# Loading the input of a nearest-neighbour upsampling as eight blocks of one 16 KiB descriptor per partition, in place of four of 32 KiB

## The chip, the cores and the metric

The kernel runs on one core of one Trainium2 chip; the other cores do nothing. The metric is the device time of an execution in microseconds (us). A kernel has two times here. The *time* is that of an execution as it was measured for the comparison (199.99 us for the kernel before, median of three runs). The *span* is what the profile of one execution covers, from the first instruction to the last (198.2 us for the same kernel); it is 1.8 us shorter.

Three words are used throughout. A *descriptor* is the order to move one contiguous run of bytes. In these traces every load and store shows one data *packet* for each descriptor, of the descriptor's size. A *semaphore* is a counter by which one unit tells another that its work is done.

## The reference

```python
x = random, shape (16, 64, 64, 64), float32; scale_factor = 2
for i in range(new_h):
    for j in range(new_w):
        result[:, :, i, j] = x[:, :, i // 2, j // 2]
```

Every element is written four times, to a square of two by two. There is no arithmetic: 16.78 MB are read, 67.11 MB are written.

## The kernel before

The input has 65,536 rows of 64 numbers. They are taken in four blocks of 128 partitions times 128 rows, each loaded with one DMA; a partition's 128 rows are contiguous in memory, 32 KiB. Each block is expanded in four steps of 32 rows. VectorE (DVE) copies 18 of the rows and ScalarE (ACT) 14, reading through a broadcast pattern that repeats rows and columns; the result, 32 KiB per partition, is stored with one DMA. There are two output buffers. All loads and all stores are issued by SyncE (SP), so they stand on one queue.

```python
K, J = 32, 4
NB = R // (P * J * K)                      # 4
xf = x.rearrange("b c h w -> (b c h) w").rearrange("(n p r) w -> n p r w", n=NB, p=P)
of = ...                                   # the same blocks of the output
KV = 18
xpool = ctx.enter_context(tc.tile_pool(name="xin", bufs=NB))
upool = ctx.enter_context(tc.tile_pool(name="uexp", bufs=2))
xts = []
for n in range(NB):
    xt = xpool.tile([P, J * K, W], fdt, name="xt")
    nc.sync.dma_start(out=xt[:, :, :], in_=xf[n])
    xts.append(xt)
...
for n in range(NB):
    for j in range(J):
        r0 = j * K
        u = upool.tile([P, K, s, W, s], fdt, name="u")
        nc.vector.tensor_copy(out=u[:, :KV], in_=expanded(xts[n][:, r0 : r0 + KV, :]))
        nc.scalar.copy(out=u[:, KV:], in_=expanded(xts[n][:, r0 + KV : r0 + K, :]))
        nc.sync.dma_start(out=of[n, :, r0 : r0 + K, :], in_=u[:, :, :, :, :])
```

A small function, `begin_before_barrier`, moves the first load ahead of the program's opening barrier. The change leaves it alone.

Of the kernel before, what the change touches and what calls it, by code (L numbers as in the profile page):

```python
# [1 line left out]

# [4 lines left out]


def begin_before_barrier(nc):



    blocks = nc.main_func.blocks
    main, body = blocks[0], blocks[1]
    sp = mybir.EngineType.SP
    load = next(i for i in body.instructions if i.engine == sp)
    assert isinstance(load, mybir.InstDMACopy), type(load)
    assert not (load.sync_info and load.sync_info.on_wait)
    body.instructions = [i for i in body.instructions if i is not load]
    kept = list(main.instructions)  # L20
    at = next(
        n
        for n, i in enumerate(kept)
        if i.engine == sp and isinstance(i, mybir.InstDrain)
    )
    kept.insert(at, load)
    main.instructions = kept


@with_exitstack  # L30
def kernel(
    ctx: ExitStack,
    tc: tile.TileContext,
    x: bass.AP,
    scale_factor: int,
    out: bass.AP,
):
    nc = tc.nc
    nc.at_finalize(begin_before_barrier)
    P = nc.NUM_PARTITIONS  # L40
    s = int(scale_factor)
    B, C, H, W = x.shape
    R = B * C * H
    fdt = x.dtype




    K, J = 32, 4
    NB = R // (P * J * K)  # L50
    assert NB * P * J * K == R
    xf = x.rearrange("b c h w -> (b c h) w").rearrange(
        "(n p r) w -> n p r w", n=NB, p=P
    )
    of = out.rearrange("b c (h hd) w -> (b c h) (hd w)", hd=s).rearrange(
        "(n p r) w -> n p r w", n=NB, p=P
    )

    KV = 18

    xpool = ctx.enter_context(tc.tile_pool(name="xin", bufs=NB))
    upool = ctx.enter_context(tc.tile_pool(name="uexp", bufs=2))

    xts = []
    for n in range(NB):
        xt = xpool.tile([P, J * K, W], fdt, name="xt")
        nc.sync.dma_start(out=xt[:, :, :], in_=xf[n])
        xts.append(xt)

    def expanded(rows):  # L70
        k = rows.shape[1]
        return rows.unsqueeze(2).unsqueeze(4).to_broadcast([P, k, s, W, s])

    for n in range(NB):
        for j in range(J):
            r0 = j * K
            u = upool.tile([P, K, s, W, s], fdt, name="u")
            nc.vector.tensor_copy(  # L78
                out=u[:, :KV], in_=expanded(xts[n][:, r0 : r0 + KV, :])
            )  # L80
            nc.scalar.copy(  # L81
                out=u[:, KV:], in_=expanded(xts[n][:, r0 + KV : r0 + K, :])
            )
            nc.sync.dma_start(
                out=of[n, :, r0 : r0 + K, :], in_=u[:, :, :, :, :]
            )


# [1 line left out]
_INS = ['x', 'scale_factor']  # L90
_OUTS = [((16, 64, 128, 128), 'float32')]

_NUMBERS = {'scale_factor': 2}


# [26 lines left out]
```

## Time and profile before

| | before |
|---|---|
| time, median of 3 runs | 199.99 us |
| span of the profiled run | 198.2 us |
| share of 16 DMA engines' span filled | 98.8% |
| DVE, ACT busy | 21%, 26% |
| data packets of the 16 engines | 2560 of 32 KiB, median 1213 ns |
| first load lands, first store issued, first store's packets start | 12.3, 15.6, 41.4 us |

These lines are from the page of the kernel before. The two rows of 40 entries cut the span into equal slices: the DMA row gives the busy share of the engines in tenths, the GB/s row what they moved. The last line is the chain of waits in shares of the span.

```profile
span 198.2 us, 145 instructions
...
DVE 40.9 (21%) x16; ACT 52.0 (26%) x17; POOL 0.2 (0%) x4
...
DMA  8999999999999999999999999999999999999994
GB/s 317 423 423 430 450 430 456 370 403 423 423 423 436 436 443 456 436 436 423 423 423 423 423 443 443 450 450 436 423 423 423 423 423 436 436 443 456 436 436 212
...
q1 hardware_dynamic: 2880, 83.89, 98.8%
...
DMA 77%; ACT 14%; issue 0%; ACTq 0%
...
```

The DMA engines are full in every slice but the first and the last. DVE and ACT are idle three quarters of the time, which speaks against either as the limit. Below is the beginning of the chain of waits in order of time: start, duration, and what the chain was in.

```profile
...
0.00 12.32 DMA xt<-in_x_dram
...
12.35 6.27 ACT u L81 x2
...
18.63 43.02 DMA out_dram<-u
...
61.75 3.19 ACT u L81
...
```

This view invites a mistake. It opens with 12.3 us of waiting for the first load and 6.3 us of copies, and one would think that a load half as large saves 5 us. But look at what follows: 43 us "in a store". Four MiB take a store only about 9.7 us of DMA. The timeline (start, duration, engine, instruction, and in brackets the idle time before it and what ended that) shows the same stretch:

```profile
...
0.00 2.15 SPq L67 DMA_DIRECT2D xt<-in_x_dram  x4
...
12.35 6.26 ACT L81 COPY u<-xt 128x3584 f32<-128x3584 f32 x2 [10.28 <-DMA xt<-in_x_dram]
...
15.55 40.05 SPq L84 DMA_DIRECT2D out_dram<-u  x3
52.07 3.18 ACT L81 COPY u<-xt 128x3584 f32<-128x3584 f32 x1 [33.47 <-DMA out_dram<-u]
...
```

The first store is issued at 15.55 us, but its buffer is free, so that the third copy can start, only at 52.07 us. It stands on the same queue behind all four loads, and those take until about 41 us. The store was ready some 26 us before the engines could turn to it. Finally, the windows view (second column: length; then busy times with counts, clock, DMA share and GB/s) of the two microseconds in which reads give way to writes:

```profile
...
39.00:41.00 2.00, 0.00 (x0) 0.00 (x0) 0.00 (x0) 1.00 0.94 262
...
```

Here the rate drops to 262 GB/s, the one dip after the start. The view counts a packet's bytes where the packet starts, and 16 packets of 32 KiB in 2 us are just 262 GB/s, so the figure is coarse.

### The profile page before, as it was taken

How to read it: one execution, taken by the hardware profiler on the slowest of the kernel's cores; microseconds unless marked ns; L12 is line 12 of the kernel's file. 1: busy time of each engine (PE TensorE's matmuls, PEld its weight loads, DVE VectorE, ACT ScalarE, POOL GpSimd, SP SyncE). 2: the span in 40 equal slices, each digit the busy share in tenths (PEclk: the TensorE clock that was granted, in tenths of full speed). 3: DMA queues.
4: the chain of work that ended last, by engine and by line, in shares of the span. 5: the costliest groups of instructions: out<-in, count | busy, mean ns of one | idle time of the engine just before them, and what ended most of it. 6: DMA issues, size and time to landing. Idle time of an engine off the chain costs nothing.

```text
span 198.2 us, 145 instructions
## 1 busy us (share of the span) xinstructions
DVE 40.9 (21%) x16; ACT 52.0 (26%) x17; POOL 0.2 (0%) x4
## 2 busy tenths in 40 slices
DVE  0055000000405050505050505050505050404000
ACT  2057000000415150606060606060606060505000
POOL 0000000000000000000000000000000000000000
DMA  8999999999999999999999999999999999999994
GB/s 317 423 423 430 450 430 456 370 403 423 423 423 436 436 443 456 436 436 423 423 423 423 423 443 443 450 450 436 423 423 423 423 423 436 436 443 456 436 436 212
DMA packets 2880, 83.89 MB, mean 423 GB/s; under 512 B 320, under 2 KB 320, under 8 KB 320
## 3 DMA queue, kind: packets, MB, share of 16 engines
q1 hardware_dynamic: 2880, 83.89, 98.8%
HBM read 16.78 MB, written 67.11 MB: 423 GB/s over the span
## 4 chain that ended last, share of the span: by engine, by line
DMA 77%; ACT 14%; issue 0%; ACTq 0%
DMA out_dram<-u 70%; ACT u L81 14%; DMA xt<-in_x_dram 6%; ACTq L81 0%
## 5 line engine op out<-in xcount | busy, mean ns | idle before, releaser
L81 ACT COPY u<-xt 128x3584 f32<-128x3584 f32 x16 | 50.8, 3179 | 128.3 <-DMA out_dram<-u 118.0
L78 DVE COPY u<-xt 128x4608 f32<-128x4608 f32 x16 | 40.9, 2560 | 139.6 <-DMA out_dram<-u 127.3
L81 ACT ACT_TABLE_LOAD x1 | 1.3, 1283 | 0.8 <-PEq L103 0.8
L103 POOL MEMSET const-bfloat16-1.0<- 128x1 bf16 x1 | 0.1, 102 | 0.0
L103 POOL MEMSET const-uint8-127<- 128x1 uint8 x1 | 0.1, 102 | 0.0
L103 POOL MEMSET const-float32-0.0<- 128x1 f32 x1 | 0.1, 99 | 0.2 <-issue 0.2
L103 POOL MEMSET const-float32-1.0<- 128x1 f32 x1 | 0.1, 99 | 0.0
## 6 DMA issues: line engine op xcount, KB each, us to landing
out_dram<-u SPq DMA_DIRECT2D x16, 4096.0 KB, 16.1
xt<-in_x_dram SPq DMA_DIRECT2D x4, 4096.0 KB, 25.9
```

The lines of the kernel that those rows point to most:

```text
L78: nc.vector.tensor_copy(out=u[:, :KV], in_=expanded(xts[n][:, r0 : r0 + KV, :]))
L81: nc.scalar.copy(out=u[:, KV:], in_=expanded(xts[n][:, r0 + KV : r0 + K, :]))
L103: nc = _bacc.Bacc("TRN2", target_bir_lowering=False, num_devices=1)
```

## The change

The intent is to start earlier: eight blocks of 64 rows per partition, each in a tile of its own, loaded with one descriptor of 16 KiB per partition. The first copies can begin after 2 MiB instead of 4 MiB. Stores, copies and the split between DVE and ACT stay as they are.

```diff
+    blocks = [64, 64, 64, 64, 64, 64, 64, 64]
-    K, J = 32, 4
-    NB = R // (P * J * K)
+    K = 32
...
+    def of_block(rows, first, k):
+        return rows[first : first + P * k, :].rearrange("(p k) w -> p k w", p=P)
-    xpool = ctx.enter_context(tc.tile_pool(name="xin", bufs=NB))
+    xpool = ctx.enter_context(tc.tile_pool(name="xin", bufs=1))
...
-    for n in range(NB):
-        xt = xpool.tile([P, J * K, W], fdt, name="xt")
-        nc.sync.dma_start(out=xt[:, :, :], in_=xf[n])
-        xts.append(xt)
+    for n, k in enumerate(blocks):
+        xt = xpool.tile([P, k, W], fdt, name=f"x{n}")
+        nc.sync.dma_start(out=xt[:, :, :], in_=of_block(xf, first, k))
+        loaded.append((xt, first, k))
+        first += P * k
...
-    for n in range(NB):
-        for j in range(J):
-            r0 = j * K
+    for xt, first, k in loaded:
+        for r0 in range(0, k, K):
...
-                out=of[n, :, r0 : r0 + K, :], in_=u[:, :, :, :, :]
+                out=of_block(of, first, k)[:, r0 : r0 + K, :],
+                in_=u[:, :, :, :, :],
```

More of the change, by code (lines that the diff above doesn't have):

```diff
@@ L44 @@
     fdt = x.dtype
-    K, J = 32, 4
-    NB = R // (P * J * K)
-    assert NB * P * J * K == R
-    xf = x.rearrange("b c h w -> (b c h) w").rearrange(
-        "(n p r) w -> n p r w", n=NB, p=P
-    )
-    of = out.rearrange("b c (h hd) w -> (b c h) (hd w)", hd=s).rearrange(
-        "(n p r) w -> n p r w", n=NB, p=P
-    )
-    KV = 18
-    xpool = ctx.enter_context(tc.tile_pool(name="xin", bufs=NB))
-    upool = ctx.enter_context(tc.tile_pool(name="uexp", bufs=2))
-    xts = []
-    for n in range(NB):
-        xt = xpool.tile([P, J * K, W], fdt, name="xt")
-        nc.sync.dma_start(out=xt[:, :, :], in_=xf[n])
-        xts.append(xt)
@@ L70, in expanded @@
-    def expanded(rows):
-        k = rows.shape[1]
-        return rows.unsqueeze(2).unsqueeze(4).to_broadcast([P, k, s, W, s])
-    for n in range(NB):
-        for j in range(J):
-            r0 = j * K
+    blocks = [64, 64, 64, 64, 64, 64, 64, 64]
+    K = 32
+    assert P * sum(blocks) == R
+    KV = 18
+    xf = x.rearrange("b c h w -> (b c h) w")
+    of = out.rearrange("b c (h hd) w -> (b c h) (hd w)", hd=s)
+    def of_block(rows, first, k):
+        return rows[first : first + P * k, :].rearrange("(p k) w -> p k w", p=P)
@@ new lines @@
+    xpool = ctx.enter_context(tc.tile_pool(name="xin", bufs=1))
+    upool = ctx.enter_context(tc.tile_pool(name="uexp", bufs=2))
+    loaded = []
+    first = 0
+    for n, k in enumerate(blocks):
[3 more added lines that the diff above has]
+        first += P * k
+    def expanded(rows):
+        return rows.unsqueeze(2).unsqueeze(4).to_broadcast(
+            [P, rows.shape[1], s, W, s]
+        )
@@ L77 @@
+    for xt, first, k in loaded:
+        for r0 in range(0, k, K):
             u = upool.tile([P, K, s, W, s], fdt, name="u")
             nc.vector.tensor_copy(
-                out=u[:, :KV], in_=expanded(xts[n][:, r0 : r0 + KV, :])
+                out=u[:, :KV], in_=expanded(xt[:, r0 : r0 + KV, :])
             )
             nc.scalar.copy(
-                out=u[:, KV:], in_=expanded(xts[n][:, r0 + KV : r0 + K, :])
+                out=u[:, KV:], in_=expanded(xt[:, r0 + KV : r0 + K, :])
```

## The prediction

> **What bounds the kernel.** The 16 DMA engines, from start to end. The page's slices show DMA at 0.8 in the first, 0.9 or more in the next 38, 0.4 in the last; the queue fills 98.8% of 16 engines' span. DVE is busy 21%, ACT 26%. Each of the 2560 data packets (512 of loads, 2048 of stores) carries 32 KiB; almost all take 1213 ns, so 160 per engine are 194.1 us of the 198.2 us span. The rest is 1.0 us before the first packet, about 0.7 us extra in each engine's first packet, about 1.0 us extra in the last two load packets, where reads give way to writes (the windows show 262 GB/s at 39 to 41 us), 0.2 us of semaphore packets (9 ns each) and 1.4 us of tail.
>
> The chain of waits seems to say otherwise: it starts with 12.3 us of the first load, then 6.3 us of ACT copies. But the stores released there stand on the same queue, behind all four loads: the first was issued at 15.6 us, started at 41.4 us when the loads had drained, and freed its buffer at 52.1 us. From there a store's 9.7 us of DMA is the period; the copies (3.18 us ACT, 2.56 us DVE) finish 6 us before the store ahead of them lands.
>
> **What the change does.** Bytes, stores, copies and buffers stay. Four loads of 32 KiB per partition become eight of 16 KiB.
> - Removed: half of the first wait. The first load lands at about 7.4 us, the first store is issued near 10.6 us. Worth nothing: it still stands behind loads that keep the queue busy until about 41 us.
> - Added: four issues on SP, 0.33 to 0.50 us each; all eight in about 4.3 us. A half load is 4.85 us of DMA, so the queue never runs dry. Hidden.
> - Added: four semaphore packets per engine, 9 ns each: 0.04 us, on the critical resource.
> - Added: 32 data packets per engine. The Trainium skill (DMA: Bandwidth & Descriptors, "Where 436 GB/s comes from") gives a ceiling of 435.2 GB/s, 1205 ns for 32 KiB on one of 16 engines; the trace has 1213 ns, and 1208 ns from start to start. So a packet's fixed cost is some 4 to 8 ns (estimate from these): 0.1 to 0.3 us.
> - Moved: a store's output runs lie 64 KiB apart between partitions, not 128 KiB, still 32 KiB long; I expect 1213 ns still.
> - Unsure: the read-to-write stretch costs 1 us in two 32 KiB packets. If it holds two packets whatever their size, up to 0.5 us may go.
>
> All of it is on the critical resource, and all is small: +0.2 us from packets, minus an uncertain 0.1.
>
> **Predicted: 200.1 us**, 199.5 to 200.8 (8 in 10). Faster by over 2%: 0.02; within 2%: 0.96; slower: 0.02.
>
> **What shows it right or wrong.** First copies start at 7 to 8 us, first store issued near 10.6 us; the third copy still starts near 52 us, the last near 178 us; DMA share stays near 98.8%; 3456 packets; load packets take 605 to 612 ns, stores 1213 ns; the first wait in the chain halves while the next DMA piece grows by the same 5 us.
>
> **What would make it wrong.** Load packets well above 612 ns; stores above 1213 ns through the new row pitch; stores overtaking the loads, so that reads and writes mix and the dip vanishes or spreads; a queue that holds fewer than eight loads, delaying the stores until DMA idles.

## The result

| | before | after |
|---|---|---|
| time, median of 4 runs each | 200.01 us (199.96 to 200.46) | 199.73 us (199.68 to 199.93) |
| span of the profiled run | 198.21 us | 198.00 us |
| first copies start | 12.35 us | 7.85 us |
| first store issued | 15.55 us | 11.05 us |
| third copies start | 52.07 us | 52.15 us |
| last copies start | 177.92 us | 177.95 us |
| last data packet ends | 196.82 us | 196.85 us |
| from there to the end of the span | 1.39 us | 1.16 us |

The ratio is 0.9983, with a 95% interval of 0.9966 to 1.0: the same at a limit of 2%, and perhaps a quarter of a microsecond faster. Ratios here are the mean time of one kernel's runs over the mean of the other's runs of the same rounds, so they are not quite the ratios of the medians in the tables. Executions over 1.5% slower than the fastest of the same kernel are left out of the means. The results are correct.

The page after:

```profile
span 198.0 us, 149 instructions
...
DMA  8999999999999999999999999999999999999995
GB/s 268 434 434 434 430 427 430 424 427 424 424 424 437 444 463 430 437 430 430 424 424 424 424 437 444 457 437 430 437 430 424 424 424 424 437 437 463 437 430 232
DMA packets 3456, 83.89 MB, mean 424 GB/s; under 512 B 384, under 2 KB 384, under 8 KB 384
...
q1 hardware_dynamic: 3456, 83.89, 99.0%
...
DMA 77%; ACT 14%; issue 0%; ACTq 0%
...
```

There are 3456 packets in place of 2880: 512 more of data and 64 more for semaphores. The engines are as full as before, and the chain's shares have hardly moved. The chain of waits in order of time:

```profile
...
0.00 7.82 DMA x<-in_x_dram
...
7.85 6.27 ACT u L83 x2
...
14.13 47.54 DMA out_dram<-u
...
61.77 3.19 ACT u L83
...
```

The first wait shrank from 12.32 to 7.82 us, and the 43.02 us in the store grew to 47.54 us. The 4.5 us that were won at the start were given back one line later. The timeline says the same:

```profile
...
0.00 4.32 SPq L68 DMA_DIRECT2D x<-in_x_dram  x8
...
7.85 6.26 ACT L83 COPY u<-x 128x3584 f32<-128x3584 f32 x2 [5.77 <-DMA x<-in_x_dram]
...
11.05 44.64 SPq L86 DMA_DIRECT2D out_dram<-u  x3
52.15 3.18 ACT L83 COPY u<-x 128x3584 f32<-128x3584 f32 x1 [38.05 <-DMA out_dram<-u]
...
```

The first store is issued 4.5 us earlier, and the third copy starts at 52.15 us, where it started at 52.07. The windows view over the same two microseconds:

```profile
...
39.00:41.00 2.00, 0.00 (x0) 0.00 (x0) 0.00 (x0) 1.00 1.00 344
...
```

Reads now give way to writes at 344 GB/s, not 262. The packet records confirm a gain in these two profiles: the last 64 KiB of loads of each engine, until its first store, took 2.89 us in place of 3.41. But the beginning was slower. In the same records, the first 2 MiB of loads took 5.73 us from the first packet until the first packet of the next 2 MiB, against 5.46 us before. The six stretches of 2 MiB between the first and the last took 4.87 us each on average, against 4.84. (From the first packets' starts: 6.74 to 35.95 us after, 6.47 to 35.51 before, divided by six.) The sum is about even. From the mean start of the 16 earliest load packets to the mean start of the 16 earliest store packets it is 40.37 us before and 40.38 us after. (A later profile of the changed kernel gave 40.16 us, so 0.2 us of this is chance. The records do not name a packet's engine; counted in another way these figures move by some hundredths, and a recorded expectation below has 40.34 and 40.17 us where this count gives 40.38 and 40.21.)

So where do the 0.2 us between the two spans come from? From the last line of the table: the last data packets end together (196.82 and 196.85 us), but the program ends 0.23 us sooner after them. The waits of SP's queue show it, as one line each (waited for whom: us in total, times, longest). Before:

```profile
...
SPq L117 <- DMA out_dram<-u: 15.7, 1, 15.7
...
```

After:

```profile
...
SPq L120 <- DMA out_dram<-u: 15.5, 2, 9.6
...
```

The line number is that of the program's end, where SP waits for the semaphores of all DMAs. Before, there was one wait for a DMA, after there are two. The records of the single waits make it plain. The DMAs take eight semaphores in rotation, and the closing waits go through them in a fixed order:

```
us, closing waits of SP
before                                     after
197.165  wait 104   (the last store's)     181.530  wait 104
197.224  wait 105, 103                     181.588  wait 105, 103
197.285  wait 106, 100                     181.650  wait 106, 100
197.349  wait 107, 99                      187.536  wait 107, 99
197.411  wait 108, 102                     197.207  wait 108, 102   (108 the last store's)
197.476  the queue's drain                 197.272  the queue's drain
```

With 20 DMAs the last store is on the fourth semaphore, number 104, which is waited for first. Everything else then follows at 0.06 us each, after the last store has landed. With 24 DMAs the last store is on the eighth, 108, which is waited for last; the other waits were over long before. Four instructions of 0.06 us (197.165 to 197.411 us) account for the difference. They have nothing to do with loads, except that there are four more of them.

### The profile page after: what moved, and what is told of

It is laid out like the page before. It is cut to its first block, busy times and chain, and to the rows that moved or that the text cites. A ratio compares the mean times of both kernels' runs of the same rounds, so it can differ in the third digit from the quotient of the medians.

```text
span 198.0 us, 149 instructions
## 1 busy us (share of the span) xinstructions
DVE 40.9 (21%) x16; ACT 52.0 (26%) x17; POOL 0.2 (0%) x4
## 2 busy tenths in 40 slices
DMA packets 3456, 83.89 MB, mean 424 GB/s; under 512 B 384, under 2 KB 384, under 8 KB 384
## 3 DMA queue, kind: packets, MB, share of 16 engines
q1 hardware_dynamic: 3456, 83.89, 99.0%
## 4 chain that ended last, share of the span: by engine, by line
DMA 77%; ACT 14%; issue 0%; ACTq 0%
DMA out_dram<-u 73%; ACT u L83 14%; DMA x<-in_x_dram 4%; ACTq L83 0%
## 5 line engine op out<-in xcount | busy, mean ns | idle before, releaser
L83 ACT COPY u<-x 128x3584 f32<-128x3584 f32 x16 | 50.8, 3179 | 128.3 <-DMA out_dram<-u 122.5
L80 DVE COPY u<-x 128x4608 f32<-128x4608 f32 x16 | 40.9, 2560 | 139.7 <-DMA out_dram<-u 131.8
```

The source lines that it names most:

```text
L80: nc.vector.tensor_copy(out=u[:, :KV], in_=expanded(xt[:, r0 : r0 + KV, :]))
L83: nc.scalar.copy(out=u[:, KV:], in_=expanded(xt[:, r0 + KV : r0 + K, :]))
```

## The experiments

The main theory has two parts. (1) The DMA engines are full, and the stores stand behind the loads; so the earlier landing is worth nothing, and the smaller descriptors come out even. (2) The 0.2 us that were won belong to the number of DMAs, through the closing waits. The rivals: the smaller descriptors, or the earlier start, made the gain; and, for (1), the order on the one queue holds back a gain that is there to be had.

Every experiment was timed in five rounds beside the kernel before on the same chip. All are correct in their results. Below, "loads" is the time from the mean start of the 16 earliest load packets to the mean start of the 16 earliest store packets, and "tail" the time from the end of the last data packet to the end of the span, both from the profiled run.

### Small descriptors without more DMAs: four_16k

The blocks of the changed kernel, loaded in pairs, so one DMA carries two 16 KiB descriptors per partition.

```diff
-        xt = xpool.tile([P, k, W], fdt, name=f"x{n}")
-        nc.sync.dma_start(out=xt[:, :, :], in_=of_block(xf, first, k))
+        xt = xpool.tile([P, 2, k, W], fdt, name=f"x{n}")
+        pair = xf[first : first + 2 * P * k, :].rearrange(
+            "(h p k) w -> p h (k w)", h=2, p=P)
+        nc.sync.dma_start(out=xt[:, :, :, :].rearrange("p h k w -> p h (k w)"), in_=pair)
```

> Four loads, but of two 16 KiB descriptors per partition each: the small descriptors without the early start and without the four more DMAs. Main theory (the 0.2 to 0.3 us by which the changed kernel is faster come from its end, where the last store's semaphore is the last and no longer the first of the queue's closing waits, because 24 and not 20 DMAs rotate over eight semaphores): load packets 611 ns, first copy at about 12.5 us, stores start at 41.3 us, tail after the last data packet 1.36 to 1.42 us as in the kernel before, span 198.2 us, time 200.0 us. Rival (the smaller descriptors made the gain): tail unimportant, time 199.7 us.

Measured: 200.11 us against 199.91, ratio 1.0014 (1.0 to 1.0028). Load packets 611 ns, first copies at 12.29 us, loads 40.30 us, tail 1.40 us, span 198.21 us. The waits of SP's queue at the program's end:

```profile
...
SPq L127 <- DMA out_dram<-u: 15.7, 1, 15.7
...
```

One wait, as before. With small descriptors alone, there is no gain in these rounds.

### More DMAs without small descriptors: eight_32k and eight_32k_b

Each load is split in two by partitions, even and odd, with 32 KiB descriptors. (Alternate partitions, and not halves: the Trainium skill, "SBUF — State Buffer", section "Door 1: The DMA port swizzle", says that the first 64 partitions reach only half of the 16 ports. By its formula, either half of alternate ones reaches all. The packets took 1213 ns as ever, which agrees; no run here tried the first 64.)

```diff
-        nc.sync.dma_start(out=xt[:, :, :], in_=xf[n])
+        for h in range(2):
+            nc.sync.dma_start(out=xt[h::2, :, :], in_=xf[n, h::2])
```

> Eight loads of 64 partitions each (even, then odd ones), still 32 KiB descriptors: the number of DMAs alone. Main theory: load packets 1213 ns, about 1 us extra in the last two rounds of load packets, stores start at 41.4 us, first copy at about 12.4 us, tail 1.15 us as in the changed kernel, span 198.0 us, time 199.75 us. Rival (smaller descriptors made the gain): 200.0 us, as before.

Measured: 200.00 us against 199.91, ratio 1.0004 (0.9992 to 1.0016). The tail was 1.15 us as the main theory expected, but the time came out as the rival had it. The trace shows why: the first data packet started at 1.32 us instead of 1.01. Everything was shifted by 0.31 us, which swallowed the 0.24 us. The experiment had changed two things. So it was made again with the first load left whole and the other three split into seven:

```diff
+        parts = [
+            [slice(0, P)],
+            [slice(0, P, 2), slice(1, P, 2)],
+            [slice(0, P, 2), slice(1, P, 2)],
+            [slice(0, P, 2), slice(1, P, 4), slice(3, P, 4)],
+        ][n]
+        for p in parts:
+            nc.sync.dma_start(out=xt[p, :, :], in_=xf[n, p])
```

> Again the number of load DMAs alone, 32 KiB descriptors kept: the first load stays whole, so that the first issue is as short as in the kernel before (in eight_32k the split one delayed the first packet by 0.31 us and hid the effect in the time); the other three are split by even and odd partitions into seven. Main theory (order of the closing waits): first packet at 1.0 us, stores start at 41.3 to 41.5 us, last data packet ends at 196.8 us, tail 1.15 us against 1.39 us, span 198.0 us, time 0.2 us below the kernel before on the same chip. Rival (the gain comes with smaller descriptors): no difference in the time, tail 1.39 us.

Measured: 199.72 us (199.60 to 199.82) against 200.00 (199.93 to 200.17), ratio 0.9986 (0.9974 to 0.9998). First packet at 0.99 us, last data packet's end at 196.78, tail 1.16 us, span 197.94 us. And at the program's end:

```profile
...
SPq L124 <- DMA out_dram<-u: 15.5, 2, 9.6
...
```

Two waits, as in the changed kernel. Its time is the changed kernel's, with the large descriptors and the late first landing of the kernel before. So the number of DMAs is enough for a gain of this size. Together with four_16k, where small descriptors without more DMAs gained nothing, that speaks for part (2) and against the rivals. The tail is also the one difference that hardly varies: in all profiles it was 1.39 or 1.40 us with 20 DMAs and 1.15 to 1.17 us with 24 or 32. No run kept the number of DMAs and moved only the last store to another semaphore, so the step from number to semaphore rests on the records of the closing waits above.

### Delaying the first landing: start_at_5 and start_at_8

The changed kernel, with the blocks worked on in another order, so that the first copy needs the fifth or the eighth load.

```diff
-    for xt, first, k in loaded:
+    for xt, first, k in loaded[4:] + loaded[:4]:      # start_at_8: 7 in place of 4
```

> The changed kernel, working on the fifth loaded block first, so the first copy has to wait for the fifth load. Main theory (the stores stand behind all loads on one queue, so the first load's landing is worth nothing as long as the first stores are issued before about 41 us): first copy at about 27 us, first store issued at about 30 us, stores still start at 41.3 us, time 199.7 us within 0.3. Rival (the time of the first store's issue counts, in part): every us of the 19 us of delay that counts is seen; over 201 us.

Measured: 199.77 us, against 199.73 of the changed kernel in its own rounds, and ratio 0.9992 (0.998 to 1.0004) to the kernel before. The timeline:

```profile
...
27.36 6.26 ACT L83 COPY u<-x 128x3584 f32<-128x3584 f32 x2 [25.30 <-DMA x<-in_x_dram]
...
30.57 25.09 SPq L86 DMA_DIRECT2D out_dram<-u  x3
52.12 3.18 ACT L83 COPY u<-x 128x3584 f32<-128x3584 f32 x1 [18.50 <-DMA out_dram<-u]
...
```

The first copies start 19.5 us later than in the changed kernel, and the third copies start at 52.12 us, as always.

> The same, working on the eighth loaded block first. Main theory: first copy at about 41.5 us, first store issued at about 44.8 us and moving from about 46 us, so DMA idles some 4 us and the time is 203 to 205 us: the slack of the first load is used up. Rival (the first load's landing never counts): 199.7 us. Rival (it counts in full): 230 us and more.

Measured: 204.99 us, ratio 1.0252 (1.0238 to 1.0265). The first store is issued at 45.07 us, after the loads have drained, and the engines stand nearly idle for five microseconds (a line of the timeline, then one of the windows view):

```profile
...
45.07 14.78 SPq L86 DMA_DIRECT2D out_dram<-u  x3
...
41.00:46.00 5.00, 4.14 (x2) 4.14 (x2) 0.00 (x0) 1.00 0.17 72
...
```

So the slack of the first landing is measured from both sides: landing at 27.3 us costs nothing, and landing at 41.8 us costs 5 us. The change moved the landing from 12.3 to 7.8 us, within the free part. (Some 0.4 to 0.6 us of the 5 is another thing: in this run the store packets had a median of 1218 ns, not 1213, and the time from the first stores to the last data packet grew by that much. Why is left open.)

### Smaller still, and a mix: sixteen_8k and mixed

```diff
-    blocks = [64, 64, 64, 64, 64, 64, 64, 64]
+    blocks = [32] * 16                                # mixed: [128, 128, 64, 64, 32, 32, 32, 32]
```

> The change taken a step further: sixteen loads of 8 KiB per partition. Theory: load packets 305 to 312 ns, so 64 more packets cost about 0.3 us; first copy at about 5.2 us, worth nothing; the stretch from reads to writes costs less again, 0.2 to 0.4 us instead of about 0.5; stores start at 41.2 to 41.6 us, tail 1.15 us as 32 DMAs end on the last of the eight semaphores again; time within 0.3 us of the kernel before. Rival (an earlier first landing or smaller loads pay): below 199.4 us.

Measured: 199.74 us, ratio 0.9989 (0.9977 to 1.0001). Load packets had a median of 309 ns, loads 40.40 us, tail 1.15 us. The stretch from reads to writes had almost nothing left to lose: the last 2 MiB of loads took 4.9 to 5.0 us until the stores, where the kernel before took 5.86 us. But the loads were slower all along: each 2 MiB between the first and the last took 4.91 to 4.98 us, not 4.84. Again what was won at the end of the loads was paid before it.

One thing in this run the expectation did not have. First copies start at 4.98 us, but the first store is issued only at 24.91 us, later than in either kernel. Sixteen loads go twice round the eight semaphores, and SP, which issues the stores too, waits before each of the last eight loads until the earlier load on the same semaphore has landed:

```profile
...
SPq L68 <- DMA x<-in_x_dram: 15.5, 8, 2.2
...
```

So this run does not try an earlier first store. It is one more in which a later one cost nothing that could be seen.

> A version meant to beat both: blocks of 128, 128, 64, 64, 32, 32, 32, 32 rows per partition, 24 DMAs. Theory: 32 KiB packets at the start (no cost of small packets there), 8 KiB packets only at the stretch from reads to writes, which then costs 0.2 to 0.4 us in place of 1.0, and the last store on the last semaphore, tail 1.15 us. Stores start at 40.7 to 40.9 us, span 197.3 to 197.5 us, time about 0.6 to 0.8 us below the kernel before. Rival (the stretch costs the same whatever the packet's size): stores start at 41.4 us, time 0.2 us below the kernel before.

Measured: 199.61 us (199.57 to 199.67) against 200.00, ratio 0.9981 (0.9969 to 0.9993). Loads 40.21 us, tail 1.15 us. Large packets first did keep the start fast (5.45 us for the first 2 MiB; 5.58 in the repeat below), but the first store packet started at 41.14 us, not at 40.7 to 40.9. The last 4 MiB, in 8 KiB packets, took 10.43 us until then (from 30.71 us), where the kernel before took 10.70 (from 30.68 to 41.37 us). So the expected gain was 0.6 to 0.8 us and about 0.4 came. It was the fastest version so far, but it had not been timed in the same rounds as the changed kernel. The last two runs did that, with both kernels as they were:

> The changed kernel itself, unedited, in the same rounds as the mix below, so that the two are compared directly. Expected: 199.7 us, 0.2 to 0.3 us below the kernel before; tail 1.15 us.

> The mix of 128, 128, 64, 64, 32, 32, 32, 32 rows once more. If its better load phase (40.17 us against 40.34 us in one profile each) is real, it is 0.1 to 0.2 us faster than the changed kernel in the same rounds, at 199.55 to 199.65 us; if not, the two are within 0.05 us of each other.

Measured: the changed kernel 199.89 us (199.85 to 200.31), ratio 0.9994 (0.998 to 1.0008) to the kernel before; the mix 199.67 us (199.64 to 199.87), ratio 0.9978 (0.9964 to 0.9992); the kernel before 200.08 us (199.92 to 200.49). So by the medians the mix beats both, by 0.2 us over the changed kernel, as expected for a real difference, and 0.4 us over the kernel before, which is a tenth and a fifth of a per cent. The tail was 1.16 us in both profiles. The loads tell nothing: 40.29 us for the mix and 40.16 for the changed kernel in these profiles, where it had been 40.21 and 40.38. One profile of the same kernel can differ from the next by 0.2 us here. Why the mix is faster than the changed kernel is therefore not shown. These runs also tell how little the 0.28 us of the first comparison weighs: on this chip the changed kernel was 0.19 us faster by its median, just short of the 0.2 to 0.3 expected, and its interval includes 1. Taken together the runs say more. In six sets of runs with 24 or 32 DMAs (the changed kernel twice, eight_32k_b, start_at_5, slow_copies and sixteen_8k) the median lay 0.05 to 0.28 us below that of the kernel before, 0.20 us on average; in four_16k, with 20, it lay 0.20 us above. (The mixes, which lay lower still, and the four runs with a delay of their own, eight_32k, start_at_8, act_queue and act_loads, are not in this count.)

### Taking the stores off the loads' queue: act_queue and act_loads

Part (1) says that the stores wait because the engines are full. The rival says that they wait because of the queue. In act_queue, the stores of the changed kernel are issued by ACT.

```diff
-            nc.sync.dma_start(
+            nc.scalar.dma_start(
                 out=of_block(of, first, k)[:, r0 : r0 + K, :],
```

> The changed kernel with its stores issued on ACT's queue, not behind the loads. Tells what makes the early first landing worthless: the order on the one queue, or the DMA engines being full. Theory (full engines): the first stores move from about 11 us on, among the loads, which therefore drain later, at 60 us or so; bytes are the same, the time stays within 199 to 202 us. Rival (the queue's order alone holds the gain back): the time falls by the 5 us of the earlier first landing or more, to 195 us or less.

Measured: 209.79 us (208.07 to 210.41), ratio 1.0487 (1.0462 to 1.0512). Neither side had expected that. The DMA row of its page, and two stretches, before and after the loads had drained at 81.0 us (length; busy times of DVE, ACT and POOL; clock; DMA share; GB/s):

```profile
...
DMA  8999999999999999999799979997999799979997
...
```

```profile
...
0.00:81.00 81.00, 14.75 (x6) 19.22 (x7) 0.20 (x4) 1.00 1.00 421
81.00:206.00 125.00, 26.12 (x11) 32.83 (x11) 0.00 (x0) 1.00 0.93 398
...
```

Up to 81 us, while loads and stores mixed, the engines moved 421 GB/s; the kernel before moved 421 GB/s in the same stretch too. The early stores did not fill anything that had been empty. The loss came later, in regular gaps. The trace shows ACT starting the copy of step 15 at 184.418 us and issuing the store of step 14 at 184.479, although that step's copy had begun at 174.72 and takes 3.18. The store's issue stood behind the next copy in ACT's own program, and that copy waits for a buffer, that is, for the store in flight to land. So the queue ran empty. That is a fault of this experiment, and the next one is free of it: the stores stay with SP, and the loads, all but the first, go to ACT.

```diff
-        nc.sync.dma_start(out=xt[:, :, :], in_=of_block(xf, first, k))
+        queue = nc.sync if n == 0 else nc.scalar
+        queue.dma_start(out=xt[:, :, :], in_=of_block(xf, first, k))
```

> The clean form of act_queue, whose stores were held up by the order of ACT's own instructions (a store's issue stood behind the next copy, which waits for a buffer): here the first load and all stores stay on SP's queue, the seven other loads go to ACT's. So the stores no longer stand behind the loads, and nothing delays their issue. Theory (the DMA engines are full whatever the order): stores and loads share the engines from about 11 us, the loads drain later, DMA stays full, time 199.4 to 201 us. Rival (the one queue's order holds the gain of the early landing back): 195 us or less.

Measured: 200.12 to 200.37 us against 199.95, ratio 1.0017 (1.0004 to 1.003). Two of its six runs were slow (203.25 and 204.58 us) and are left out.

```profile
span 198.6 us, 147 instructions
...
DMA  8999999999999989999999999999999999999995
...
```

```profile
...
13.42 52.58 SPq L87 DMA_DIRECT2D out_dram<-u  x5
33.36 3.18 ACT L84 COPY u<-x 128x3584 f32<-128x3584 f32 x1 [16.89 <-DMA out_dram<-u]
...
```

The first store is issued at 13.42 us and its buffer is free at 33.36 us, 19 us before the changed kernel's. (The first load landed at 10.19 us here and not at 7.82, where ACT's loads ran beside it from 4.6 us on.) The loads then last until 90.25 us. The time is the same within 2%, and some 0.4 us worse. So it isn't the queue that makes the early start worthless; the engines are full either way. The Trainium skill ("DMA: Bandwidth & Descriptors", section "Issuing engines are not separate DMA queues") says that DMAs of several issuing engines end up on the same 16 DMA engines and interleave. This run agrees: between 20 and 88 us, by the packet records, SP's queue moved 288 GB/s and ACT's 144, which is 433 in all, as ever. The ratio of two to one is that of the packets' sizes. The section "Queues, rings and completion order" of the same page has each DMA engine take its queues in turn; an equal number of packets from each gives just this ratio, and 591 packets of SP's queue and 593 of ACT's started in this stretch. After how many packets an engine switches can't be told from these rates.

### Are the copies on the critical path? slow_copies

The chain of waits puts 14% of the span down to ACT's copies. In this version ACT copies 28 of the 32 rows.

```diff
-    KV = 18
+    KV = 4
```

> The changed kernel with 28 of the 32 rows of each copy on ACT and 4 on DVE, not 14 and 18: ACT copies of about 6.4 us in place of 3.18. The chain of waits puts 14% of the span down to these copies. Theory (a copy ends 6 us before the store ahead of it lands, so it is hidden): first store issued at about 14.3 us, time 199.7 us within 0.3. Rival (the chain is to be taken at its word, with nine copies on it): about 29 us more.

Measured: 199.90 us, ratio 0.9995 (0.9983 to 1.0008). Timeline and page:

```profile
...
52.29 6.17 ACT L83 COPY u<-x 128x7168 f32<-128x7168 f32 x1 [32.27 <-DMA out_dram<-u]
...
61.91 6.17 ACT L83 COPY u<-x 128x7168 f32<-128x7168 f32 x1 [3.45 <-DMA out_dram<-u]
...
```

```profile
span 198.1 us, 149 instructions
...
```

Copies of 6.17 us, twice as long, change nothing that these rounds can tell from 0. The idle time before them shrank by as much as they grew: before the copy at 61.91 us it is 3.45 us, and in the changed kernel it was 6.44:

```profile
...
61.77 3.18 ACT L83 COPY u<-x 128x3584 f32<-128x3584 f32 x1 [6.44 <-DMA out_dram<-u]
...
```

That is how slack looks.

## Why the prediction was right

The prediction was 200.1 us, within 199.5 to 200.8; measured were 199.73 us. It was right, and its main reason was shown; one small term was missing. The range, 1.3 us wide, would have held a small effect of either sign, so the time alone is a weak test: the marks that follow are the stronger one.

- *The DMA engines bound the kernel, and the landing is worth nothing*: right, and shown. Nineteen microseconds of delay cost nothing (start_at_5); when the delay outlasts the loads, it costs (start_at_8). Taking the stores off the queue does not bring the gain out (act_loads).
- *First copies at 7 to 8 us, first store issued near 10.6 us, third copy near 52 us, the last near 178 us; the first wait halves and the next piece of the chain grows by as much*: right (7.85, 11.05, 52.15, 177.95 us; 12.32 to 7.82 and 43.02 to 47.54 us), with the first store 0.4 us later than foreseen.
- *Eight issues hidden, in 4.3 us*: right. They took 4.32 us, and the DMA row shows no empty slice.
- *Load packets 605 to 612 ns, a packet's fixed cost 4 to 8 ns*: the packets right, the fixed cost slightly too small. They took 611 ns. Two of them are 1222 ns where one of 32 KiB is 1213, so each packet more costs 9 ns by these medians, and 32 more on each engine are 0.29 us. The estimate rested on the ceiling of 435.2 GB/s that the Trainium skill states ("DMA: Bandwidth & Descriptors", section "Where 436 GB/s comes from"); the trace's steady 433 GB/s lies just below it.
- *Stores at 1213 ns in spite of the new pitch of their rows*: right.
- *The stretch from reads to writes, "up to 0.5 us may go"*: right in kind. The last 64 KiB of loads of each engine, and what came until the first store, took 3.41 us before and 2.89 after: 0.5 us less. But other runs with 16 KiB packets won between 0.3 and 0.7 us there, and the start lost about 0.3 us in return, which the prediction did not have. Whether smaller packets lose at the start in general is open: four_16k, whose first DMA was of 4 MiB, did not (5.40 us for the first 2 MiB), while start_at_5 did (5.78 us).
- *The sum, +0.1 us*: wrong in sign. The packets' side came out at zero or slightly below (loads 40.38 us, and 40.16 in a later profile, against 40.37). The missing term was the tail, which the prediction carried as 1.4 us and took for fixed. It depends on which of the eight semaphores the last store happens to use, and it fell from 1.39 to 1.16 us. eight_32k_b, which has the shorter tail without smaller packets, ran 0.28 us below the kernel before, as the changed kernel had.

## What to carry to other kernels

When one resource is full from end to end, a shorter first wait only lengthens the next one; ask what the released work will stand behind before counting a wait as a gain. A chain of waits shows what released what, not what would be saved: the test of a wait is to lengthen it, and the point where the time begins to follow is its slack. And when two versions differ by a tenth of a per cent, look at the first and the last microsecond before giving the credit to the idea.

## What the Trainium skill lacked or had wrong

- "DMA: Bandwidth & Descriptors" gives no time for a data packet of HWDGE by its size. Here a median of 309 ns for 8 KiB, 611 ns for 16 KiB and 1213 ns for 32 KiB were measured on each of 16 engines.
- No page that was read says that the engines lose time when a full queue turns from loads to stores. Here it was 0.8 to 1.0 us with 32 KiB packets (in the kernel before 3.41 us for the last two packets of each engine, of which 2.42 were due at the steady pace) and 0.3 to 0.7 us with 16 KiB packets.
- "SBUF — State Buffer", in its rules for kernel authors, advises one DMA and not several when a transfer is DMA-bound. Here splitting loads of 4 MiB, queued one behind the other, from four into eight cost nothing that could be seen: eight_32k_b took 199.72 us and the kernel before 200.00, and the difference is about that of the closing waits (0.23 us).
- No page that was read mentions that the end of a program depends on which semaphore the last DMA uses: 1.39 or 1.40 us after the last data packet with 20 DMAs, 1.15 to 1.17 us with 24 or 32, at 0.06 us for each wait that is left.
- No page that was read tells why store packets stayed slower in a run whose stores began after an idle stretch, a median of 1218 ns a packet in start_at_8 against 1213.
